# The second layer's mixer of an fp32 block net in a written order, with PSUM tiles and more weights prepared ahead

## Chip, cores, metric

One core of a Trainium2 chip (trn2). The metric is the device time of one execution of the program in microseconds; lower is better.

## What is computed

The input x is 256 tokens by 1024 channels, in fp32. A first block has two layers, each a mixer and an MLP with a residual, and a second block with two kinds of attention follows. The change touches the MLP of the first layer (called MLP 0) and the mixer of the second (called layer 1), so only these are shown:

```python
def rg_lru(x, w_r, b_r, w_i, b_i, lam):
    r = sigmoid(einsum("bshi,hij->bshj", xb, w_r) + b_r)   # 8 heads of 128
    i = sigmoid(einsum("bshi,hij->bshj", xb, w_i) + b_i)
    log_a = -8 * r * softplus(-lam)
    a = exp(log_a)
    bx = sqrt(-expm1(2 * log_a)) * (i * x)
    return scan over tokens of h = a * h_before + bx

def mixer_c(h, w_in, conv_w, conv_b, w_r, b_r, w_i, b_i, lam, w_out):
    gate, xr = split(h @ w_in, 2)
    xr = causal_depthwise_conv(xr, conv_w) + conv_b        # 4 taps
    y = rg_lru(xr, ...) * gelu(gate)
    return y @ w_out

def sq_relu_mlp(h, w_up, w_down):
    return square(relu(h @ w_up)) @ w_down
```

Ahead of a mixer and an MLP stands an RMS norm of x.

## The kernel before

**Products.** Channels lie on partitions, tokens on the free axis. Each fp32 operand is a high half (rounded to the engine's fp32r) and a low half (the rest), and a product is three matmuls of 128x128 by 128x256 (`mm3`): high weight by high input (L360), high weight by low input (L361), low weight by high input (L362).

**Weight units.** The weights are 243 units of 128x1024 (512 KB) in the order in which PE uses them (`weight_plan`, L70). SP issues their transfers into four tiles `raw`, one after the other; a transfer waits until the unit four before has been read for the last time. `ready` (L312) and `prep` (L304) then make the high half (a copy on ACT, L307, or on DVE, L309) and the low half (a subtraction on DVE or POOL, L310). `POLICY` (L44) names the two engines by kind of unit, "a", "v" and "g" for ACT, DVE and POOL: "ag" is the high half on ACT and the low half on POOL. The halves go into a ring of `RING` = 6 buffers `wh` and `wl` and, between layer 0 and the middle of MLP 1, `EXTRA` = 4 more, `wxh` and `wxl`. `unit(name, ahead)` (L341) hands out the next unit and prepares so many beyond it as `ahead` says: 2, and from step 10 of MLP 0 on `FAR` = 6. Each engine executes its own instructions in order; a scheduler places them where the program leaves it free, so that in layer 1 pieces of several products are interleaved on PE.

**MLP 0** has 16 steps: an up product of 256 columns, relu and square, and from the third step on two rows of the down product. Its last rows and its end are `proj_tail` (L818): for each of four column blocks the last 4 rows, the residual x, its high half scaled by the gain (`xsh`, ACT, L841), its low half (`xsl`, DVE, L847) and its square (L855); the squares are added up in `s1` (DVE, L857), and POOL folds the two halves of `s1` (L861).

**Layer 1** (`layer1`, L987) has 26 units of 24 matmuls: 8 `xr`, 2 `ri` (the gates' weights of four heads each), 8 `cg` (the gelu branch), 8 `wo1` (the output, one row of 128 input channels each). `gfirst` (L376) multiplies the first four xr units; between, two columns of matmuls sum `s1` over partitions (L424), and POOL computes the inverse root `rc` (L435) from which PE and ACT spread `R` over the partitions (L442, L448). The two halves of the squares' sum are needed there. The product with R gives xr (DVE, L1034); ACT starts the convolution (L1038), DVE adds three taps (L1042), the last into an SBUF tile `xc`, and each head is split into `xch` (ACT, L399) and `xcl` (DVE, L407) in two buffers. `ri(u)` multiplies them; ACT makes the two gates (L1018, L1019) from a PSUM tile `acc`, and then a second tanh and the decay's exponential (L1022, L1023); DVE squares the decay (L1026). Then come the root (L1057), the gelus (L1050), DVE's scans (L1064), the product with the gelu (L1066) and the split of the result into `xr` (ACT, L399) and `ysl` (DVE, L407), and the output rows. Its first five rows are multiplied row by row, the last three in `proj_tail`. The scheduler is held by one rule only: roots after the last exponential, gelus after the roots (`issue_after`).

Of the kernel before, what the change touches and what calls it, by code (L numbers as in the profile page):

```python
# [17 lines left out]
T = 256  # L18
# [9 lines left out]
EXTRA = 4  # L28
FAR = 6
# [15 lines left out]
POLICY.update(val=("av", "ag", "av", "ag"), gate=("av", "av", "av", "ag"), xr=("av", "ag"), ri=("vg",), cg=("vg",))  # L45
POLICY["wo0"] = ("ag",) * 7 + ("av",)
POLICY["up"] = ("ag",) * 4 + ("av",) * 60
POLICY["wo1"] = ("ag",) * 2 + ("av",) * 6
# [21 lines left out]
def weight_plan(I):  # L70
# [48 lines left out]
    ri(1)  # L119
    for j in range(8):  # L120
        inn("cg", w, j * 128)
# [127 lines left out]
class Kern:  # L249
# [11 lines left out]

    def pool(self, name, space=None):
        return self.tc.tile_pool(name=name, bufs=1) if space is None else \
            self.tc.tile_pool(name=name, bufs=1, space=space)
# [47 lines left out]
    def ready(self):  # L312
# [26 lines left out]
        self.q.append((name, (wh, wl)))  # L339

# [477 lines left out]
    def proj_tail(self, acc, name, ins, gname, g0, xs, R2=None, mp=None, sums=(), after=None):  # L818
# [4 lines left out]
        with self.tc.issue_after(after.ins) if after else nullcontext():  # L823
            ws = [self.unit(name) for _ in ins]
        n = len(ins)
        late = []
        for b in range(4):
# [17 lines left out]
            if xs is not None:  # L845
                for k in ks:
                    V.scalar_tensor_tensor(xs[1][:, k], x[:, k], g[k % 2], xs[0][:, k].bitcast(F32),  # L847
                                           op0=ALU.mult, op1=ALU.subtract)
            for i, (st, scaled) in enumerate(sums):
# [10 lines left out]
        for st, _ in sums:  # L860
            G.tensor_tensor(st[:, 0], st[:, 0], st[:, 1], op=ALU.add)  # L861

    def mod_setup(self, mp):
# [4 lines left out]
        tv = self.t(mp, [128, 2048], "tv")  # L868
# [118 lines left out]
    def layer1(self, lp):  # L987
# [8 lines left out]
        xc = self.t(lp, [128, 8, T], "xc")  # L996
# [4 lines left out]
        parts = [self.s1[:, 0]]  # L1001
        rc = []
        self.ahead = 2
# [3 lines left out]
        def ri(u):  # L1007
            w = self.unit("ri")
            hs = range(4 * u, 4 * u + 4)
            for h in hs:  # L1010
                xch = self.t(lp, [128, T], "xch", F32R, bufs=2)
                xcl = self.t(lp, [128, T], "xcl", F32R, bufs=2)
                self.split(xc[:, h], xch, xcl)
                ps = self.ps("acc")
                for i in range(2):
                    c = slice(((h % 4) * 2 + i) * 128, ((h % 4) * 2 + i + 1) * 128)
                    self.mm3(ps[:, i * T:(i + 1) * T], (w[0][:, c], w[1][:, c]), (xch, xcl), True, True)
                S.activation(r[:, h], ps[:, :T], AF.Tanh, bias=hb[:, h:h + 1], scale=0.5)  # L1018
                S.activation(ig[:, h], ps[:, T:], AF.Tanh, bias=hb[:, 8 + h:9 + h], scale=0.5)  # L1019
                V.scalar_tensor_tensor(ig[:, h], ig[:, h], 1.0, xc[:, h], op0=ALU.add, op1=ALU.mult)  # L1020
            for h in hs:
                S.activation(th[:, h], r[:, h], AF.Tanh, scale=sp[:, h:h + 1], bias=sp[:, h:h + 1])  # L1022
                last = S.activation(r[:, h], r[:, h], AF.Exp, scale=nsp[:, h:h + 1], bias=nsp[:, h:h + 1])  # L1023
                if h % 2:
                    sl = slice(h - 1, h + 1)
                    V.tensor_tensor(xc[:, sl], r[:, sl], r[:, sl], op=ALU.mult)  # L1026
                    V.scalar_tensor_tensor(th[:, sl], xc[:, sl], 1.0, th[:, sl], op0=ALU.add, op1=ALU.mult)
            return last

        for p in range(4):  # L1030
            if 2 * p == RI0:
                ri(0)
            ps = pss[p] if p < 2 else self.gpair(("xr", "xr"), xs)
            V.tensor_tensor(xr[:, 2 * p:2 * p + 2, 3:], self.pair(ps), self.b2(R), op=ALU.mult)  # L1034
            ca = self.pair(self.ps("acc"))
# [3 lines left out]
            for i in range(3):  # L1039
                for h in range(2):  # L1040
                    j = 2 * p + h
                    V.scalar_tensor_tensor(xc[:, j] if i == 2 else ca[:, h], xr[:, j, i:i + T],  # L1042
                                           self.p("ccw", j * 4 + i), ca[:, h], op0=ALU.mult, op1=ALU.add)

        def gate_pair(p):
            ps = self.gpair(("cg", "cg"), xs)
            xg = gl[:, 2 * p:2 * p + 2]
            V.tensor_tensor(xg, self.pair(ps), self.b2(R), op=ALU.mult)
            with self.tc.issue_after(sq.ins):
                S.activation(xg, xg, AF.Gelu_apprx_tanh)  # L1050

        ex = ri(1)
        ys = (self.t(lp, [128, 8, T], "xr", F32R), ysl)
        sls = [slice(4 * b, 4 * b + 4) for b in range(2)]
        for sl in sls:
            with self.tc.issue_after(ex.ins):
                sq = S.activation(th[:, sl], th[:, sl], AF.Sqrt, scale=0.25)  # L1057
        for p in range(4):
            gate_pair(p)
        for b, sl in enumerate(sls):  # L1060
            V.tensor_tensor(ig[:, sl], ig[:, sl], th[:, sl], op=ALU.mult)
            for p in (2 * b, 2 * b + 1):
                for h in (2 * p, 2 * p + 1):
                    V.tensor_tensor_scan(xc[:, h], r[:, h], ig[:, h], 0.0, op0=ALU.mult, op1=ALU.add)  # L1064
                hp = slice(2 * p, 2 * p + 2)
                V.tensor_tensor(xc[:, hp], xc[:, hp], gl[:, hp], op=ALU.mult)  # L1066
                self.split(xc[:, hp], ys[0][:, hp], ys[1][:, hp])
        acc = [self.ps("acc") for _ in range(4)]
        for k in range(5):
            self.krow(acc, self.unit("wo1"), (ys[0][:, k], ys[1][:, k]), k == 0, False)  # L1070
        xs = self.new_h()
# [462 lines left out]
```

## Time and profile before

| what | us |
|---|---|
| median of 3 executions | 831.25 |
| lowest, highest | 829.29, 834.26 |
| the profiled execution | 829.35 |
| its span | 827.5 |

Of the span PE (matmul) was busy 790.3 us, 96%; DVE 71%, ACT 55%, POOL 27%. The mean granted clock of TensorE was 0.987 of full speed. The rows below are of that execution; times count from the start of its span. MLP 0 ends and layer 1 begins on PE at 292 us, and layer 1 ends at 385 us. A row of a table by stretch names the stretch, then for each engine its busy time and the number of its instructions. A row of waits names the engine and line that waits, what it waits for, and how long.

### The profile page before, as it was taken

The numbers are of one execution on the slowest core, as the hardware profiler recorded it, in microseconds if no ns is written. First come the engines' busy times: TensorE is split into PE (matmuls) and PEld (weight loads), VectorE is DVE, ScalarE is ACT, GpSimd is POOL, SyncE is SP. The second block draws the span as 40 slices with busy tenths as digits, with TensorE's granted clock in tenths as the row PEclk, the third lists the DMA queues.
The fourth block names the chain that finished last, engine by engine and source line by source line (L and its number), as shares of the span: only waits on it lengthen the run. The fifth ranks groups of instructions, "written<-read, shape, count | busy, mean of one in ns | idle before, by whom it ended". The sixth has DMA issues, their size and how long they took to land.

```text
span 827.5 us, 16152 instructions
## 1 busy us (share of the span) xinstructions
PE 790.3 (96%) x6476; PEld 757.8 (92%) x6476; DVE 589.2 (71%) x956; ACT 457.4 (55%) x722; POOL 220.6 (27%) x160
## 2 busy tenths in 40 slices
PE   6999899999999978798999999999999999999996
PEld 6997799999999978698999999999989988889996
DVE  6899659999997698898638445557634877566743
ACT  5578546544446625576636444545626587765433
POOL 4886634110111465500441101111000022220001
PEclk9999999999999999799999999999999999999998
DMA  7864357878878744318646566665234532554621
GB/s 237 305 204 128 102 179 240 336 269 301 289 275 280 250 120 136 112 49 303 222 126 202 185 183 201 191 194 177 85 126 142 165 104 101 179 166 166 204 78 51
DMA packets 41259, 152.32 MB, mean 184 GB/s; under 512 B 4576, under 2 KB 5088, under 8 KB 39008
## 3 DMA queue, kind: packets, MB, share of 16 engines
q1 hardware_dynamic: 40752, 149.19, 55.4%
q10 hardware_dynamic: 432, 2.10, 0.6%
q8 instruction: 51, 0.84, 0.4%
q14 instruction: 24, 0.20, 0.1%
HBM read 149.17 MB, written 2.10 MB: 183 GB/s over the span
## 4 chain that ended last, share of the span: by engine, by line
PE 74%; DVE 11%; ACT 5%; DMA 3%; issue 3%; POOL 2%; SPq 0%; POOLq 0%; DVEq 0%; ACTq 0%
PE mm L360 13%; PE mm L361 13%; PE mm L362 12%; PE acc L361 10%; PE acc L360 9%; PE acc L362 9%; DMA raw<-in_wst 3%; PE acc L1320 2%; PE acc L1348 2%; PE mm L1357 2%; DVE wl L310 2%; ACT wh L307 1%; DVE ysl L407 1%; POOL wl L310 1%; PE mm L442 1%
## 5 line engine op out<-in xcount | busy, mean ns | idle before, releaser
L307 ACT ACTIVATE wh<-raw 128x1024 fp32r<-128x1024 f32 (+1 forms) x198 | 207.1, 1049 | 185.6 <-PE mm L361 77.3
L310 DVE TENSOR_TENSOR wl<-raw,wh 128x1024 fp32r<-128x1024 f32 (+1 forms) x167 | 208.8, 1257 | 109.5 <-ACT wh L307 109.4
L361 PE MATMUL mm<-xsl,wh 128*128 128x256 f32 x824 | 229.7, 279 | 1.5 <-DVE xsl L847 1.5
L360 PE MATMUL mm<-xsh,wh 128*128 128x256 f32 x824 | 231.0, 280 | 0.0
L362 PE MATMUL mm<-xsh,wl 128*128 128x256 f32 x824 | 229.6, 279 | 0.0
L360 PEld LDWEIGHTS mm<-xsh,wh 128*128 128x128 f32 x824 | 156.0, 189 | 3.7 <-issue 3.3
L361 PEld LDWEIGHTS mm<-xsl,wh 128*128 128x128 f32 x824 | 156.0, 189 | 2.6 <-DVE xsl L847 2.1
L362 PEld LDWEIGHTS mm<-xsh,wl 128*128 128x128 f32 x824 | 155.6, 189 | 0.0
L957 POOL TENSOR_TENSOR ma<-mr 128x512 f32<-128x512 f32 x32 | 49.7, 1554 | 233.7 <-ACT mr L955 233.7
L361 PE MATMUL acc<-mal,wh 128*128 128x256 f32 x384 | 106.6, 278 | 0.7 <-DVE mal L407 0.7
L360 PE MATMUL acc<-mah,wh 128*128 128x256 f32 x384 | 106.7, 278 | 0.0
L362 PE MATMUL acc<-mah,wl 128*128 128x256 f32 x384 | 106.3, 277 | 0.0
L310 POOL TENSOR_TENSOR wl<-raw,wh 128x1024 fp32r<-128x1024 f32 x36 | 87.9, 2463 | 27.9 <-ACT wh L307 27.2
L361 PEld LDWEIGHTS acc<-mal,wh 128*128 128x128 f32 x384 | 72.4, 188 | 1.3 <-DVE mal L407 1.3
L362 PEld LDWEIGHTS acc<-mah,wl 128*128 128x128 f32 x384 | 72.1, 188 | 0.0
L360 PEld LDWEIGHTS acc<-mah,wh 128*128 128x128 f32 x384 | 72.1, 188 | 0.0
L307 ACT ACTIVATE wxh<-raw 128x1024 fp32r<-128x1024 f32 x35 | 36.6, 1056 | 34.7 <-DMA raw<-in_wst 27.0
L883 DVE CUSTOM_DVE_ANT_0 mdump<-mw,cv 128x1024 f32<-128x1024 f32 x40 | 51.0, 1274 | 3.4 <-DMA mw<-in_modw 3.1
L310 DVE TENSOR_TENSOR wxl<-raw,wxh 128x1024 fp32r<-128x1024 f32 x34 | 43.7, 1305 | 9.4 <-ACT wxh L307 9.4
L361 PE MATMUL mm<-xsl,wxh 128*128 128x256 f32 x168 | 47.5, 283 | 1.9 <-DVE xsl L847 1.9
L360 PE MATMUL mm<-xsh,wxh 128*128 128x256 f32 x168 | 47.6, 284 | 0.2 <-ACT xsh L841 0.2
L362 PE MATMUL mm<-xsh,wxl 128*128 128x256 f32 x168 | 47.2, 281 | 0.0
(374 smaller groups left out, 1765.1 us busy)
## 6 DMA issues: line engine op xcount, KB each, us to landing
raw<-in_wst SPq DMA_DIRECT2D x240, 512.0 KB, 4.1
mw<-in_modw SPq DMA_DIRECT2D x12, 1024.0 KB, 7.5
nb<-in_nab SPq DMA_DIRECT2D x16, 256.0 KB, 3.6
ab<-in_alibi ACTq DMA_DIRECT2D x1, 1536.0 KB, 7.8
x<-in_xT SPq DMA_DIRECT2D x4, 256.0 KB, 5.2
cv<-in_cvec SPq DMA_DIRECT2D x1, 1024.0 KB, 4.7
cx<-in_cT SPq DMA_DIRECT2D x1, 1024.0 KB, 6.5
xd<-x SPq DMA_DIRECT2D x1, 1024.0 KB, 4.4
```

The costliest lines, as they stand in the source:

```text
L307: nc.scalar.activation(wh, r, AF.Copy)
L310: (nc.vector if lo == "v" else nc.gpsimd).tensor_tensor(wl, r, wh.bitcast(F32), op=ALU.subtract)
L360: mm(out, w[0], x[0], start=start, stop=False, skip_group_check=True)
L361: mm(out, w[0], x[1], start=False, stop=False, skip_group_check=True)
L362: return mm(out, w[1], x[0], start=False, stop=stop, skip_group_check=True)
L407: self.nc.vector.tensor_tensor(l, src, h.bitcast(F32), op=ALU.subtract)
L442: self.lasts = self.nc.tensor.matmul(ps[:, j * 128:(j + 1) * 128], rc[:, j:j + 1].to_broadcast([128, 128]), self.ident, start=True, stop=True)
L883: V.tensor_tensor_reduce(d, w, cv[:, s * 1024:(s + 1) * 1024], 0.5, 0.0, op0=ALU.mult, op1=ALU.add, accum_out=self.mod[:, s * 24 + i:s * 2 ...
L957: G.tensor_tensor(a, r, r, op=ALU.mult)
L1320: PE.matmul(sc[i], Q[tag, h][a][:, qs], K[tag, h][b], start=a + b == 0, stop=a == 1)
L1348: PE.transpose(pt[:, i * 128:(i + 1) * 128], P[:, i * 128:(i + 1) * 128], self.ident)
L1357: PE.matmul(o[64 * hh:64 * hh + 64, :T], vt[:, i, h * 64:h * 64 + 64], PTs[tag, h][:, i], start=i == 0, stop=i == 3, skip_group_check=True)
```

## The change

- `EXTRA` goes from 4 to 6 buffers and `FAR` from 6 to 11 units, so that up to eleven units can be ready when MLP 0 ends. In the tail the units are taken with fewer ahead, and `fill(n)`, a new function that prepares until n units are waiting, sets how many are prepared at each place.
- `ri` and every second `cg` and `wo1` change engines: all 26 high halves of layer 1 are ACT's. The second `ri` unit stands behind the first two cg units.
- POOL's fold of `s1` is left out in MLP 0, and the sum over partitions takes both halves (4 matmuls of one column instead of 2).
- `layer1` is written as steps in a fixed order. `inorder` chains each PE and each ACT instruction of layer 1 to the one before it, so the scheduler can't exchange them. The convolved heads stay in the PSUM tiles `acc` (no `xc`), `xch` and `xcl` have four buffers, the gates' products go into `mm` tiles, the decay is squared by ACT into PSUM, root and gelu come in two halves (5 table loads instead of 2).

```diff
-EXTRA = 4
-FAR = 6
+EXTRA = 6
+FAR = 11
...
-POLICY.update(val=("av", "ag", "av", "ag"), gate=("av", "av", "av", "ag"), xr=("av", "ag"), ri=("vg",), cg=("vg",))
+POLICY.update(val=("av", "ag", "av", "ag"), gate=("av", "av", "av", "ag"), xr=("av", "ag"), ri=("ag",), cg=("ag", "av"))
...
-POLICY["wo1"] = ("ag",) * 2 + ("av",) * 6
+POLICY["wo1"] = ("ag", "av")
...
-    ri(1)
     for j in range(8):
+        if j == 2:
+            ri(1)
         inn("cg", w, j * 128)
...
+    @contextmanager
+    def inorder(self, *engines):
+
+        traced = self.nc.cur_bb.bb.instructions
+        old = {id(i) for i in traced}
+        yield
+        last = {}
+        for i in traced:
+            if id(i) not in old and i.engine in engines:
+                if i.engine in last:
+                    self.tc.add_manual_dep(i, last[i.engine].name, mybir.DependencyInfo(
+                        mybir.DependencyClass.NoSync, mybir.DependencyReason.DATA), reason="issue_after")
+                last[i.engine] = i
...
+    def fill(self, n):
+
+        while len(self.q) < n and self.u < N_UNITS:
+            self.ready()
...
-            ws = [self.unit(name) for _ in ins]
+            ws = [self.unit(name, len(ins) - 1 - i) for i in range(len(ins))]
...
+            self.fill(min(1 + b, 3))
...
-        for st, _ in sums:
+        for st, _ in sums if mp and xs is None else ():
...
-        tv = self.t(mp, [128, 2048], "tv")
+        tv = self.t(mp, [128, 2048], "mw", bufs=2)
...
-        xc = self.t(lp, [128, 8, T], "xc")
...
-        parts = [self.s1[:, 0]]
+        parts = [self.s1[:, 0], self.s1[:, 1]]
         rc = []
-        self.ahead = 2
+        self.ahead = 0
+        PIN = (PE.engine, S.engine)
...
-            ca = self.pair(self.ps("acc"))
+            ca = cas[p] = self.pair(self.ps("acc"))
...
-                    V.scalar_tensor_tensor(xc[:, j] if i == 2 else ca[:, h], xr[:, j, i:i + T],
+                    V.scalar_tensor_tensor(ca[:, h], xr[:, j, i:i + T],
...
+        def heads(p):
+            for h in (2 * p, 2 * p + 1):
+                sp3[h] = (self.t(lp, [128, T], "xch", F32R, bufs=4), self.t(lp, [128, T], "xcl", F32R, bufs=4))
+                self.split(cas[p][:, h % 2], *sp3[h])
+
+        def ri(u):
+            w = self.unit("ri")
+            out = []
+            for h in range(4 * u, 4 * u + 4):
+                ps = self.ps()
+                for i in range(2):
+                    c = slice(((h % 4) * 2 + i) * 128, ((h % 4) * 2 + i + 1) * 128)
+                    self.mm3(ps[:, i * T:(i + 1) * T], (w[0][:, c], w[1][:, c]), sp3[h], True, True)
+                out.append(ps)
+            return out
+
+        def gates(u, pr):
+            for h in range(4 * u, 4 * u + 4):
+                ps = pr[h % 4]
+                S.activation(r[:, h], ps[:, :T], AF.Tanh, bias=hb[:, h:h + 1], scale=0.5)
+                S.activation(ig[:, h], ps[:, T:], AF.Tanh, bias=hb[:, 8 + h:9 + h], scale=0.5)
+                V.scalar_tensor_tensor(ig[:, h], ig[:, h], 1.0, cas[h // 2][:, h % 2], op0=ALU.add, op1=ALU.mult)
+
+        def tanhs(u):
+            for h in range(4 * u, 4 * u + 4):
+                S.activation(th[:, h], r[:, h], AF.Tanh, scale=sp[:, h:h + 1], bias=sp[:, h:h + 1])
+
+        def decay(p):
+            for h in (2 * p, 2 * p + 1):
+                S.activation(r[:, h], r[:, h], AF.Exp, scale=nsp[:, h:h + 1], bias=nsp[:, h:h + 1])
+            sl = slice(2 * p, 2 * p + 2)
+            a2 = self.pair(self.ps("acc"))
+            S.activation(a2, r[:, sl], AF.Square)
+            V.scalar_tensor_tensor(th[:, sl], a2, 1.0, th[:, sl], op0=ALU.add, op1=ALU.mult)
+
+        def root(u):
+            sl = slice(4 * u, 4 * u + 4)
+            S.activation(th[:, sl], th[:, sl], AF.Sqrt, scale=0.25)
+            for p in (2 * u, 2 * u + 1):
+                hp = slice(2 * p, 2 * p + 2)
+                V.tensor_tensor(ig[:, hp], ig[:, hp], th[:, hp], op=ALU.mult)
+                for h in (2 * p, 2 * p + 1):
+                    V.tensor_tensor_scan(th[:, h], r[:, h], ig[:, h], 0.0, op0=ALU.mult, op1=ALU.add)
+
...
+
+        def gelu(p):
+            S.activation(gl[:, 2 * p:2 * p + 2], gl[:, 2 * p:2 * p + 2], AF.Gelu_apprx_tanh)
+
+        def done(p):
+            hp = slice(2 * p, 2 * p + 2)
+            V.tensor_tensor(th[:, hp], th[:, hp], gl[:, hp], op=ALU.mult)
+            self.split(th[:, hp], ys[0][:, hp], ys[1][:, hp])
+
+        def wrow(k):
             self.krow(acc, self.unit("wo1"), (ys[0][:, k], ys[1][:, k]), k == 0, False)
+
+        with self.inorder(*PIN):
+            conv(0, pss[0])
+            self.fill(5)
+            conv(1, pss[1])
+            self.fill(6)
+            p2 = self.gpair(("xr", "xr"), xs)
+            heads(0)
+            heads(1)
+            r0 = ri(0)
+            self.fill(5)
+            conv(2, p2)
+            gates(0, r0)
+            self.fill(7)
+            tanhs(0)
+            p3 = self.gpair(("xr", "xr"), xs)
+            self.fill(7)
+            conv(3, p3)
+            decay(0)
+            self.fill(8)
+            decay(1)
+            cg(0)
+            heads(2)
+            heads(3)
+            self.fill(8)
+            gates(1, ri(1))
+            root(0)
+            self.fill(8)
+            cg(1)
+            ys = (self.t(lp, [128, 8, T], "xr", F32R), ysl)
+            gelu(0)
+            gelu(1)
+            done(0)
+            tanhs(1)
+            self.fill(8)
+            cg(2)
+            done(1)
+            decay(2)
+            decay(3)
+            self.fill(8)
+            cg(3)
+            root(1)
+            gelu(2)
+            gelu(3)
+            self.fill(7)
+            acc = [self.ps("acc") for _ in range(4)]
+            for k in range(4):
+                wrow(k)
+                self.fill(7)
+            done(2)
+            done(3)
+            wrow(4)
+        self.ahead = 2
```

Three places show how the instructions move.

POOL, from the end of MLP 0 on. `wxl` and `wl` are low halves of weights, `s` is `s1`, `rc` the inverse root. Before:

```order
L310 TENSOR_TENSOR wxl_3590<-raw_3587,wxh_3589 128x1024
L310 TENSOR_TENSOR wxl_3881<-raw_3878,wxh_3880 128x1024
L995 MEMSET xr_3739 128x8x3
L310 TENSOR_TENSOR wl_3951<-raw_3948,wh_3950 128x1024
L861 TENSOR_TENSOR s_5_76<-s_5_76 128x256
L310 TENSOR_TENSOR wl_4026<-raw_4023,wh_4025 128x1024
L310 TENSOR_TENSOR wl_4056<-raw_4053,wh_4055 128x1024
L435 TENSOR_TENSOR rc_3820<-var_3818,mhalf_85 128x2
L310 TENSOR_TENSOR wl_4096<-raw_4093,wh_4095 128x1024
```

After:

```order
L978 TENSOR_TENSOR ma_3524<-mr_3523 128x512
L325 TENSOR_TENSOR wxl_3568<-raw_3565,wxh_3567 128x1024
L1016 MEMSET xr_3744 128x8x3
L455 TENSOR_TENSOR rc_3826<-var_3824,mhalf_85 128x2
L325 TENSOR_TENSOR wxl_3882<-raw_3879,wxh_3881 128x1024
L325 TENSOR_TENSOR wxl_3898<-raw_3895,wxh_3897 128x1024
```

Ahead of `rc` stood five low halves and the fold, now one low half; those of xr 7 and of the first cg unit come behind it.

PE at the first product of `ri(0)`. `mm` tiles of `xsh`, `xsl` are the xr product, `xch` and `xcl` the convolved heads. Before:

```order
L360 MATMUL mm_618_4022<-xsh_557_3567,wh_604_3950 128x256
L361 MATMUL mm_618_4022<-xsl_558_3568,wh_604_3950 128x256
L362 MATMUL mm_618_4022<-xsh_557_3567,wl_605_3951 128x256
L361 MATMUL acc_608_3958<-xcl_607_3955,wxh_597_3880 128x256
L362 MATMUL acc_608_3958<-xch_606_3954,wxl_598_3881 128x256
L360 MATMUL acc_608_3958<-xch_606_3954,wxh_597_3880 128x256
L361 MATMUL acc_608_3958<-xcl_607_3955,wxh_597_3880 128x256
L362 MATMUL acc_608_3958<-xch_606_3954,wxl_598_3881 128x256
L361 MATMUL acc_611_3972<-xcl_610_3969,wxh_597_3880 128x256
L362 MATMUL acc_611_3972<-xch_609_3968,wxl_598_3881 128x256
```

After:

```order
L380 MATMUL mm_606_3901<-xsh_572_3597,wxh_564_3533 128x256
L381 MATMUL mm_606_3901<-xsl_573_3598,wxh_564_3533 128x256
L382 MATMUL mm_606_3901<-xsh_572_3597,wxl_565_3534 128x256
L380 MATMUL mm_615_3966<-xch_607_3950,wxh_569_3567 128x256
L381 MATMUL mm_615_3966<-xcl_608_3951,wxh_569_3567 128x256
L382 MATMUL mm_615_3966<-xch_607_3950,wxl_570_3568 128x256
```

Before, the first matmul of head 0 went out ahead of others of xr 6, and the rest followed between them; now the heads come in one piece right behind xr 5, and xr 6 and 7 behind all four heads.

ACT at the end of layer 1. `th` and `gl` are the roots and gelus, `xr` from `th` the split of the result, two channel rows of wo1 each. Before:

```order
L1057 ACT_TABLE_LOAD
L1057 ACTIVATE th_3744<-th_3744 128x1024 x2
L1050 ACT_TABLE_LOAD
L1050 ACTIVATE gl_3746<-gl_3746 128x512 x3
L307 ACTIVATE wh_4480<-raw_4478 128x1024
L399 ACTIVATE xr_4167<-xc_3742 128x512
L307 ACTIVATE wh_4510<-raw_4508 128x1024
L399 ACTIVATE xr_4167<-xc_3742 128x512
L307 ACTIVATE wh_4540<-raw_4538 128x1024
L307 ACTIVATE wxh_4570<-raw_4568 128x1024
L399 ACTIVATE xr_4167<-xc_3742 128x512
L1050 ACTIVATE gl_3746<-gl_3746 128x512
L399 ACTIVATE xr_4167<-xc_3742 128x512
```

After:

```order
L322 ACTIVATE wxh_4399<-raw_4397 128x1024
L322 ACTIVATE wh_4405<-raw_4403 128x1024
L1079 ACT_TABLE_LOAD
L1079 ACTIVATE th_3748<-th_3748 128x1024
L1091 ACT_TABLE_LOAD
L1091 ACTIVATE gl_3750<-gl_3750 128x512 x2
L322 ACTIVATE wh_4470<-raw_4468 128x1024
L322 ACTIVATE wh_4504<-raw_4502 128x1024
L322 ACTIVATE wh_4534<-raw_4532 128x1024
L322 ACTIVATE wh_4564<-raw_4562 128x1024
L322 ACTIVATE wh_4594<-raw_4592 128x1024
L419 ACTIVATE xr_4312<-th_3748 128x512 x2
```

Before, one or two high halves stood between two splits; now five stand in one piece between the last gelus and the splits for rows 4 to 7.

## Rows read from the trace of the kernel before

**Rows 1.** Busy time by stretch: layer 1, and its last part without pauses.
```profile
core 0: us, PE busy (x) PEld busy (x) DVE busy (x) ACT busy (x) POOL busy (x), PEclk, DMA share, GB/s
292.00:385.00 93.00, 79.75 (x632) 77.11 (x631) 80.62 (x107) 48.62 (x83) 35.63 (x16) 0.93 0.43 133
349.00:385.00 36.00, 35.97 (x318) 35.77 (x317) 30.42 (x40) 24.86 (x33) 0.00 (x0) 1.00 0.42 138
```

**Rows 2.** Waits of PE, 280 to 385 us: total, times, longest.
```profile
PE acc L361 <- DVE xcl L407: 7.7, 4, 5.1
PE mm L442 <- POOL rc L435: 3.0, 1, 3.0
PE mm L361 <- DVE xsl L847: 1.5, 1, 1.5
PE mm L424 <- POOL s L861: 0.6, 1, 0.6
```

**Rows 3.** Busy time by stretch, columns as in rows 1: behind two pauses.
```profile
310.00:315.00 5.00, 5.00 (x33) 5.00 (x31) 2.26 (x4) 2.58 (x5) 5.00 (x3) 0.66 0.52 165
345.00:350.00 5.00, 5.00 (x33) 5.00 (x33) 2.71 (x5) 4.28 (x10) 0.00 (x0) 0.70 0.13 47
```

**Rows 4.** Timeline of POOL: start, length, operation, [idle before <- releaser].
```profile
302.23 5.61 POOL L310 TENSOR_TENSOR wl<-raw,wh 128x1024 fp32r<-128x1024 f32 x2
307.80 1.68 POOL L435 TENSOR_TENSOR rc<-var,mhalf 128x2 f32<-128x2 f32 x1
317.04 2.40 POOL L310 TENSOR_TENSOR wxl<-raw,wxh 128x1024 fp32r<-128x1024 f32 x1 [0.68 <-issue]
```

**Rows 5.** Timeline of DVE, columns as in rows 4.
```profile
292.73 4.64 DVE L847 SCALAR_TENSOR_TENSOR xsl<-x,par,xsh 128x256 fp32r<-128x256 f32 x2
320.36 0.68 DVE L1034 TENSOR_TENSOR xr<-mm,R 128x512 f32<-128x512 f32 x1
338.12 0.48 DVE L1042 SCALAR_TENSOR_TENSOR acc<-xr,par,acc 128x256 f32<-128x256 f32 x1
338.51 2.17 DVE L407 TENSOR_TENSOR xcl<-xc,xch 128x256 fp32r<-128x256 f32 x1
358.61 1.85 DVE L1064 TENSOR_TENSOR_SCAN xc<-r,ig 128x256 f32<-128x256 f32 x3
372.08 1.23 DVE L310 TENSOR_TENSOR wxl<-raw,wxh 128x1024 fp32r<-128x1024 f32 x1
```

**Rows 6.** Timeline of ACT, columns as in rows 4.
```profile
310.36 0.39 ACT L448 ACTIVATE R<-mm 128x256 f32<-128x256 f32 x1 [10.97 <-PE mm L442]
321.07 1.17 ACT L1038 ACTIVATE acc<-xr,par 128x256 f32<-128x256 f32 x2 [0.58 <-DVE xr L1034]
330.01 0.47 ACT L1018 ACTIVATE r<-acc,hb 128x256 f32<-128x256 f32 x1
330.36 0.48 ACT L1019 ACTIVATE ig<-acc,hb 128x256 f32<-128x256 f32 x1
333.80 2.00 ACT L307 ACTIVATE wh<-raw 128x1024 fp32r<-128x1024 f32 x2
352.23 1.09 ACT L1023 ACTIVATE r<-r,sm 128x256 f32<-128x256 f32 x2
353.34 1.28 ACT L1057 ACT_TABLE_LOAD   x1
354.63 2.01 ACT L1057 ACTIVATE th<-th 128x1024 f32<-128x1024 f32 x2
357.96 1.68 ACT L1050 ACTIVATE gl<-gl 128x512 f32<-128x512 f32 x3
```

**Rows 7.** DMA issues: times, KB each, median us to landing.
```profile
raw<-in_wst SPq DMA_DIRECT2D x240, 512.0 KB, 4.1
```

**Rows 8.** Busy time by stretch, columns as in rows 1: the end of MLP 0.
```profile
250.00:280.00 30.00, 30.00 (x267) 30.00 (x266) 20.03 (x18) 20.95 (x24) 9.51 (x5) 1.00 0.84 272
```

**Rows 9.** Waits of PE, 385 to 400 us, columns as in rows 2.
```profile
PE mm L361 <- DVE xsl L847: 1.9, 3, 0.9
```

## What the change will do to the time, and why

> **What bounds the kernel now.** The page's first part comes first; by it PE is the engine that is busy nearly all the time, so time can only be won where PE pauses or runs at the lower clock. The table of busy time by stretch then shows where: in layer 1, from 292 to 385 us, PE issued 632 matmuls, was busy 79.75 of 93.00 us, and the granted clock was 0.93; in the stretch 349 to 385 it issued 318 in 36 us without a pause, 0.113 us each [rows 1]. Layer 1 has 26 weight units of 24 matmuls, 624, which is 70.6 us at that pace; the few small ones of the norm take another 0.9. So 93.0 - 71.5 = 21.5 us are lost there. PE's waits name 12.8 of them: 7.7 for the low half of the convolved heads (`xcl`), 3.0 for `rc`, 1.5 for the low half of the residual (`xsl`) and 0.6 for the fold `s` [rows 2]. After the 3.0 us wait the clock was 0.66 for five microseconds, 33 matmuls where 44 would fit; after the 5.1 us wait the same is seen again in 345 to 350 [rows 3]. That is the clock's lower level (1.2 instead of 2.4 GHz) after a pause. It cost 11 x 0.113 = 1.3 us the first time and about twice that the second, 4 in all. The rest, 4.7 us, is short gaps.
>
> What is late in these waits? POOL's rows: two low halves queued (5.61 us) ahead of `rc` [rows 4]. DVE's rows: two `xsl` of 128x256 took 4.64 us while POOL ran low halves, and one `xcl` 2.17 us, where an operation with its operand in PSUM, the convolution's tap, took 0.48 beside POOL [rows 5]. So layer 1 waits for DVE and POOL hindering each other, and for POOL's order.
>
> **What the change takes away.** At the start of layer 1 POOL has no low half and no fold of the square sums left, only the memset and `rc`. The waits for `xsl` (1.5), for the fold (0.6) and for `rc` (3.0) go, and with the last the 1.3 at the lower clock: 6.4 us. The convolved heads now stay in PSUM and most low halves are done elsewhere: the `xcl` waits (7.7) and the 2.7 at the lower clock go: 10.4 us. The short gaps sat between interleaved pieces that no longer exist; I count their 4.7 as gone. Together 21.5 us.
>
> **What it costs: new waits, because PE and ACT are pinned.** ACT now makes all high halves, the squares, and five table loads instead of two, in a written order, and PE cannot pull other work forward. I walk ACT and DVE through that order with the durations of [rows 5, 6]: gate tanhs start 0.36 apart, second tanhs and exponentials 0.5 (1.09 for two), conv starts 1.17 a pair, high halves 1.0, gelus 0.56 and the splits of the same tile 0.6, square roots 1.0, loads 1.28.
> (a) `ri(0)` stands right behind xr 4 and 5. From R to the first `xcl`: R 0.4, product 0.68, conv starts 1.17, high half 1.0, low half 1.23, six taps 2.4, `xch` 0.4, then two taps, a product and `xcl` 1.8: 9.1 us with the hand-overs; PE has 48 matmuls, 5.4. Wait 3.7, and 1.1 more for the other heads: 4.8.
> (b) xr 6 and 7 need a PSUM tile that `ri(0)` holds until its first gates; ACT has two high halves, two conv starts and two gates ahead, 4.0, PE 1.2: 2.7.
> (c) `ri(1)` needs `xch` of head 4, behind 7 gates 2.5, five high halves 5.0, 4 tanhs 2.0, conv starts 1.17, exponentials 2.0, squares 1.2, split 0.4: 14.3, against 96 matmuls, 10.9. With `xcl` and the next heads 4.6.
> (d) cg 2 waits like (b): 2.8 against 1.1, 1.7.
> (e) wo1's first row needs a tile that DVE frees after the second decay, 2.3.
> (f) wo1's row 4 needs `done(2)`'s split. ACT from the gate of head 4: 7 gates 2.5, five loads 6.4, square roots 2.0, gelus 2.2, tanhs and exponentials 4.0, squares 1.1, five high halves 5.0, two splits 1.2: 24.4; in it a wait of 2.9 for DVE's four scans (0.62 each), products and a low half. Behind the last gelu stand five more high halves. The fifth can't start before the raw tile of the first is free: high half 1.0, low half on POOL 2.4 [rows 4], transfer 4.1 [rows 7], high half 1.0, low half on DVE 1.2, `ysl` 0.7: 10.4. Together 37.7 us; PE has 240 matmuls, 27.1, and (e): 29.4. Wait 8.3.
> Sum 24.4 us. At the lower clock I add 2.0: after 3.0 us of pause 1.3 was lost, after 5.1 us 2.7 [rows 3]; what follows (a) is swallowed by (b), what follows (f) isn't. So layer 1 loses 26.4 instead of 21.5: +4.9.
>
> **Beside it.** At MLP 1's start PE now waits 1.9 for `xsl` [rows 9], because the first up units arrive there late; after the change seven lie ready, and I take 1.9 and a small gap of 0.2 as gone (other end: they stay, nothing won). The five more units prepared in MLP 0 need 2.6 MB over the 65 us from 215 to 280, 40 GB/s beside 272 at a DMA share of 0.84 [rows 8], and 3 DVE low halves; SP issues their transfers in the one queue of the weights, each when the raw tile four units back is free. At that pace a full share would be 272 / 0.84 = 324, so 52 are free for the 40. PE waits for nothing there, so I cost them at nothing. If that cover fails, the cost is rival 4 below. Two more matmuls of one column in the norm: under 0.3 us.
>
> **The sum**: 829.35 (the profiled execution; 1.9 under the median of 831.25) + 4.9 - 2.1 = 832.1. The forecast is 832.0, no change that can be told (0.5% is 4.2 us). Its own range is 828.5 to 835.5.
>
> A page of the Trainium skill speaks against this change: ScalarE: Activation LUTs, section What ACT_TABLE_LOAD costs, gives about 1.28 us for a load and 1.38 for a drain at every switch. The row has 1.28 for the load, and the square root begins at 354.63, 0.01 after the load's end [rows 6], so the trace shows no drain; by the page the five loads would cost 6.9 more, and the sum would be 839.0.
>
> **The rivals.**
> 1. ACT arrives early, **faster**. If ACT reaches its last gelu 8 us sooner than my chain says, (f) and the lower clock behind it vanish: 832.1 - 8.3 - 2.0 = 821.8. For it: ACT was busy only 48.6 of 93 us [rows 1]; 12 more high halves, 3 loads and 4 squares make it 67, so it has room, and my chains let every link start as late as possible. Against it: the chain of (f) is bound by one raw tile, a POOL low half and a transfer, each measured. Each microsecond that ACT gains is one for the kernel, down to that value.
> 2. The lower clock, **slower**. If the pause before `ri(0)` acts like the one of 5.1 us, PE runs xr 6 and 7 at half pace: 48 x 0.113 = 5.4 us later for conv 3, which stands in ACT's pinned chain with about one microsecond to spare. Then everything up to (f) shifts by 4.4, and the sum is 836.5. [...] For it: three pauses of over 3 us follow one another; against it: (b) covers half of the first.
> 3. Each table load stops ACT for as long again as the load itself: five times 1.28 = 6.4 in chain (f), 838.5. Against it are the 0.01 us between load and square root. The page named above has this rule.
> 4. MLP 0 can't prepare eleven units, because the transfers are near what they do: then layer 1 starts with few, POOL and DVE meet again in the transition, and the 6.4 come back: 838.5. Against it are the 52 GB/s free.
>
> **How the numbers follow.** Forecast 0.38, rival 1 0.30, rival 2 0.23, rival 3 0.04, rival 4 0.05. Faster is rival 1, 0.30; slower are the last three and the upper edge of the forecast, 0.34; 0.36 remains for no change. The range goes from 820 (rival 1 less a little) to 839 (rivals 3 and 4); it leaves out the tails of the two large cases, two in ten.
>
> **What would show it.** Right: no PE wait for `rc` or `xsl` in the transition, `R` made at about 304 us instead of 310.4 [rows 6]; pauses of 3 to 5 us at the first matmul with `xch` and `xcl`; the largest pause, 6 to 9 us, on the split of wo1's rows 4 and 5 with ACT's fifth high half waiting for a transfer; MLP 1 starting at 387 to 391. Wrong: a pause on POOL in the transition (rival 4), a gap behind each table load (rival 3), clock under 0.7 between 310 and 335 (rival 2), or no pause at wo1's row 4 (rival 1).

## Result and profile after

| | before | after |
|---|---|---|
| median, us | 831.03 (20 executions) | 836.95 (20 executions) |
| lowest, highest | 826.25, 834.74 | 831.30, 842.31 |
| the profiled execution, its span | 829.35, 827.5 | 838.86, 837.1 |

The change makes the kernel slower: 5.9 us, a ratio of 1.007 with an interval of 1.0052 to 1.0089. The first part of the page of the kernel after:

```profile
span 837.1 us, 16157 instructions
PE 793.6 (95%) x6480; PEld 761.5 (91%) x6480; DVE 576.5 (69%) x946; ACT 473.9 (57%) x739; POOL 213.9 (26%) x157
```

The two profiled executions are 9.6 us of span apart, the medians 5.9, since one profile lies 1.9 above its median and the other 1.7 below. Where the 9.6 arise is read from the starts of the same matmuls in both traces. 1.9 are there before the order differs anywhere, so they are chance. MLP 0 adds 6.4 between its second and its last down row. From that last row to the first down row of MLP 1 it is 113.44 us against 113.27: **layer 1 and the start of MLP 1 together add only 0.2**. Behind it come another 1.2, and then nothing more. So the loss lies in a stage that I had priced at nothing, and the rewritten layer breaks even.

The waits of PE from 236 to 397 us after the change (engine, line, what it waits for: total, times, longest), which answer to [rows 2]:

```profile
PE acc L380 <- ACT xr L419: 5.5, 1, 5.5
PE mm L380 <- ACT xch L419: 4.6, 2, 2.4
PE acc L381 <- DVE mal L427: 3.1, 2, 2.7
PE mm L381 <- DVE xcl L427: 2.4, 2, 1.5
PE mm L380 <- ACT ig L1062: 2.4, 1, 2.4
PE acc L380 <- DVE th L1075: 2.2, 2, 1.6
PE acc L381 <- DVE ysl L427: 0.8, 1, 0.8
```

`rc`, `s` and `xsl` have gone, as was foretold, also at the start of MLP 1 [rows 9]. In their place stand waits for the pinned chains, 17.9 us without `mal`. `mal`, the low half of MLP 0's squared relu, is new at this size. In the same view of before it has this row:

```profile
PE acc L361 <- DVE mal L407: 0.2, 1, 0.2
```

Busy time by stretch after the change, columns as in [rows 1]; the first answers to [rows 8], and the last two to [rows 3]:

```profile
250.00:280.00 30.00, 30.00 (x257) 30.00 (x256) 21.48 (x24) 19.62 (x22) 9.67 (x6) 1.00 0.78 263
289.00:293.00 4.00, 3.94 (x20) 3.94 (x21) 1.30 (x3) 0.00 (x0) 0.00 (x0) 0.57 0.46 135
320.00:325.00 5.00, 3.66 (x21) 2.89 (x22) 3.66 (x9) 2.30 (x5) 1.94 (x1) 1.00 0.65 218
345.00:350.00 5.00, 5.00 (x36) 5.00 (x35) 3.11 (x6) 4.98 (x11) 2.50 (x1) 0.77 0.35 108
385.00:390.00 5.00, 5.00 (x32) 5.00 (x32) 3.46 (x4) 2.87 (x3) 0.00 (x0) 0.68 0.96 318
```

The granted clock is the mean of a stretch. It falls to its lower level (1.2 GHz) for a part of the stretches behind the `mal` wait (289), behind the second pause of the heads (345) and behind the one of row 4 (385), but not behind `ri(0)`'s pauses (320 to 325, 1.00).

**The wait at the end of MLP 0.** The timeline of POOL after the change, there and late in layer 1 (start, length, operation, [idle before <- releaser]):

```profile
282.18 2.98 POOL L325 TENSOR_TENSOR wxl<-raw,wxh 128x1024 fp32r<-128x1024 f32 x1 [0.37 <-ACT wxh L322]
285.12 1.04 POOL L978 TENSOR_TENSOR ma<-mr 128x512 f32<-128x512 f32 x1
286.12 2.34 POOL L325 TENSOR_TENSOR wxl<-raw,wxh 128x1024 fp32r<-128x1024 f32 x1
...
375.73 2.49 POOL L325 TENSOR_TENSOR wl<-raw,wh 128x1024 fp32r<-128x1024 f32 x1 [4.34 <-ACT wh L322]
```

The timeline of ACT, the same columns, at that place, at R and ahead of row 4:

```profile
282.01 0.58 ACT L976 ACTIVATE mr<-mm 128x512 f32<-128x512 f32 x1
...
312.83 0.39 ACT L468 ACTIVATE R<-mm 128x256 f32<-128x256 f32 x1 [9.11 <-PE mm L462]
...
372.25 1.28 ACT L1091 ACT_TABLE_LOAD   x1
373.54 1.16 ACT L1091 ACTIVATE gl<-gl 128x512 f32<-128x512 f32 x2
374.61 3.89 ACT L322 ACTIVATE wh<-raw 128x1024 fp32r<-128x1024 f32 x4
381.67 1.06 ACT L322 ACTIVATE wh<-raw 128x1024 fp32r<-128x1024 f32 x1 [3.18 <-DMA raw<-in_wst]
382.63 1.14 ACT L419 ACTIVATE xr<-th 128x512 fp32r<-128x512 f32 x2
```

The timeline of DVE, the same columns, in the middle of MLP 0 and at its end:

```profile
242.08 1.22 DVE L904 CUSTOM_DVE_ANT_0 mdump<-mw,cv 128x1024 f32<-128x1024 f32 x1 [4.38 <-DMA mw<-in_modw]
...
286.20 2.81 DVE L427 TENSOR_TENSOR mal<-ma,mah 128x512 fp32r<-128x512 f32 x1 [3.30 <-POOL ma L978]
```

The last of these rows, as it was at the same place before:

```profile
281.65 0.69 DVE L407 TENSOR_TENSOR mal<-ma,mah 128x512 fp32r<-128x512 f32 x1 [3.30 <-POOL ma L957]
```

The last relu `mr` is ready at 282.59. POOL could square it then, but a low half (`wxl`, of a unit prepared for layer 1) stands in front and holds POOL until 285.16: 2.6 us. The square's low half `mal` is DVE's and starts at 286.20, while POOL has begun the next low half, and takes 2.81 instead of the 0.69 before. PE's timeline shows the outcome, and the pauses of layer 1 with it:

```profile
289.06 0.45 PE L381 MATMUL acc<-mal,wxh 128*128 128x256 f32 x1 [2.70 <-DVE mal L427]
...
320.36 0.38 PE L380 MATMUL mm<-xch,wxh 128*128 128x256 f32 x1 [2.19 <-ACT xch L419]
321.65 0.38 PE L381 MATMUL mm<-xcl,wxh 128*128 128x256 f32 x1 [0.91 <-DVE xcl L427]
321.87 0.29 PE L382 MATMUL mm<-xch,wxl 128*128 128x256 f32 x1
321.99 0.28 PE L380 MATMUL mm<-xch,wxh 128*128 128x256 f32 x1
...
383.30 0.58 PE L380 MATMUL acc<-xr,wxh 128*128 128x256 f32 x1 [5.48 <-ACT xr L419]
```

Against before, by the starts of the same matmuls, that is 2.5 us of gap and 1.6 behind it at the lower clock. The rest of the 6.4 in MLP 0 is not of the same certainty: DVE waited 4.38 us for the modulation's data, with `mal` behind it in the queue, PE paused 0.4 at 245 and lost 0.7 there in all, and from there to 286 its matmuls came 0.118 us apart instead of 0.1135 (257 in 30 us instead of 267), 1.5 us.

A page of the Trainium skill bears on `mal`: GPSIMD Engine Reference, section 1. Specifications, says that POOL shares its SBUF interfaces with VectorE, with contention for DVE instructions that have two SBUF inputs. The trace agrees: 2.81 us against 0.69, and `mal` has two.

### The profile page after: what moved, and what is told of

The parts are those of the page before. It is cut to its first block, busy times and chain, and to the rows that moved or that the text cites. A ratio compares the mean times of both kernels' runs of the same rounds, so it can differ in the third digit from the quotient of the medians.

```text
span 837.1 us, 16157 instructions
## 1 busy us (share of the span) xinstructions
PE 793.6 (95%) x6480; PEld 761.5 (91%) x6480; DVE 576.5 (69%) x946; ACT 473.9 (57%) x739; POOL 213.9 (26%) x157
## 4 chain that ended last, share of the span: by engine, by line
PE 52%; ACT 5%; DVE 5%; issue 2%; POOL 1%; DMA 0%; POOLq 0%; DVEq 0%; ACTq 0%
PE mm L380 9%; PE mm L381 9%; PE mm L382 9%; PE acc L381 6%; PE acc L382 6%; PE acc L380 6%; PE acc L1402 2%; PE acc L1430 2%; PE mm L1439 2%; ACT wh L322 1%; DVE wl L325 1%; ACT wxh L322 1%; DVE acc L1039 1%; PE mm L462 1%; ACT th L1067 0%
## 5 line engine op out<-in xcount | busy, mean ns | idle before, releaser
L380 PE MATMUL mm<-xsh,wh 128*128 128x256 f32 x808 | 225.9, 280 | 0.0
L381 PE MATMUL mm<-xsl,wh 128*128 128x256 f32 x808 | 224.4, 278 | 0.0
L382 PE MATMUL mm<-xsh,wl 128*128 128x256 f32 x808 | 224.3, 278 | 0.0
L381 PE MATMUL acc<-mal,wh 128*128 128x256 f32 x360 | 100.2, 278 | 1.0 <-DVE mal L427 1.0
L380 PE MATMUL acc<-mah,wh 128*128 128x256 f32 x360 | 100.4, 279 | 0.0
L382 PE MATMUL acc<-mah,wl 128*128 128x256 f32 x360 | 100.0, 278 | 0.0
L325 POOL TENSOR_TENSOR wl<-raw,wh 128x1024 fp32r<-128x1024 f32 x33 | 79.7, 2433 | 46.0 <-ACT wh L322 40.8
L322 ACT ACTIVATE wxh<-raw 128x1024 fp32r<-128x1024 f32 x48 | 50.4, 1058 | 40.8 <-DMA raw<-in_wst 36.3
L381 PEld LDWEIGHTS acc<-mal,wh 128*128 128x128 f32 x360 | 68.0, 189 | 1.2 <-DVE mal L427 1.2
L325 DVE TENSOR_TENSOR wxl<-raw,wxh 128x1024 fp32r<-128x1024 f32 x41 | 53.5, 1313 | 7.1 <-ACT wxh L322 6.7
```

The lines of the kernel that those rows point to most:

```text
L322: nc.scalar.activation(wh, r, AF.Copy)
L325: (nc.vector if lo == "v" else nc.gpsimd).tensor_tensor(wl, r, wh.bitcast(F32), op=ALU.subtract)
L380: mm(out, w[0], x[0], start=start, stop=False, skip_group_check=True)
L381: mm(out, w[0], x[1], start=False, stop=False, skip_group_check=True)
L382: return mm(out, w[1], x[0], start=False, stop=stop, skip_group_check=True)
```

## Experiments

The theory behind the first runs (A, where an expectation uses letters): the loss is made in MLP 0, by low halves that the longer preparation puts on POOL ahead of the last squares, and layer 1 only exchanges waits. Its rival: layer 1's written order makes the loss, by ACT's chain.

**1. The last low halves of MLP 0 on DVE** (after, with two units' engines changed):

```diff
-xr=("av", "ag"), ri=("ag",),
+xr=("av", "ag", "av", "ag", "av", "av", "av", "ag"), ri=("av", "ag"),
```

> The low halves of xr 5 and of the first ri unit, the last two that MLP 0 prepares, go from POOL to DVE; nothing else changes. Theory A (POOL's low halves stand ahead of the last `ma` of MLP 0, and PE waits 2.7 us for it and then runs at the lower clock): the wait for `mal` at the end of MLP 0 falls from 2.7 to under 0.5 us, the stretch at half clock behind it (1.3 us) is gone, the time falls by about 4 us, to 833. Theory B (the loss lies in layer 1's pinned order, the wait in MLP 0 was one of the profiled execution): no change, 837. Theory C (the added units' transfers come late, whoever makes the low half): the wait for `mal` stays at 1.5 us or more, now behind DVE's low halves, 836.

Measured: 832.63, ratio 1.002 [0.9999, 1.0040]. POOL's rows at the same place:

```profile
278.37 2.41 POOL L325 TENSOR_TENSOR wl<-raw,wh 128x1024 fp32r<-128x1024 f32 x1 [0.57 <-ACT wh L322]
282.17 1.72 POOL L978 TENSOR_TENSOR ma<-mr 128x512 f32<-128x512 f32 x1 [1.40 <-ACT mr L976]
```

POOL is idle when the last relu comes, and the wait at 286 is gone. In ratio the loss falls from 0.7% to 0.2%: two entries of a table undo 4 to 5 of the 5.9 us. One wait for `mal` is left in PE's waits from 236 to 397 us:

```profile
PE acc L381 <- DVE mal L427: 1.2, 1, 1.2
```

It is the pause at 245, longer here than in after, with the pace of 0.118 us behind it, and MLP 0 is still 3.2 us longer than before's in this profile. POOL's low halves at the end of MLP 0 don't make that pause. Run 2, which differs from after in layer 1 alone, doesn't have it in its profile, nor does run 6; there MLP 0 is 6.2 and 6.3 us longer by the wait at its end and the lower clock behind it. What makes the pause at 245 was not tried.

**2. The last two results finished before the output rows** (after):

```diff
             acc = [self.ps("acc") for _ in range(4)]
+            done(2)
+            done(3)
             for k in range(4):
                 wrow(k)
                 self.fill(7)
-            done(2)
-            done(3)
```

> The two splits for wo1's rows 4 to 7 are written ahead of the four preparations that stand between rows 0 to 3; nothing else changes. If the wait at row 4 is the chain of the prediction's term (f) (high half, low half on POOL, transfer, high half, split), the waits of 5.5 and 0.8 us at row 4 fall to under 2 in all and the 1.5 us at the lower clock behind them go: 6 less in layer 1. Part comes back at MLP 1's start, whose first units are then prepared later: net 3 to 6 less, 831 to 834. Rival: all of it comes back there, because the units' transfers are the limit: 836 to 837.

Measured: 834.23, ratio 1.0037 [1.0013, 1.0060], just above the 831 to 834 expected. The wait at row 4 fell from 5.5 to 1.6 us, MLP 0 still had its `mal` wait (3.6).

**3. Both** (edits 1 and 2).

> Both edits of the two runs before. If they are independent the gains add up: 8 us less, 829, about 2 us below the kernel before. If only theory B holds, as the second run alone; if only A, as the first.

Measured: 830.59, ratio 0.9983 [0.9963, 1.0003]. The two gains add, within the intervals. With these two places mended, what is left is neither faster nor slower than before.

**4. The preparation undone in after.**

```diff
-FAR = 11
+FAR = 6
```

> FAR back from 11 to 6, the rest as in the changed kernel. Theory A: MLP 0's end is as in the kernel before (no wait for `mal` over 0.5 us, no half clock: 5 to 6 us less there), but four or five units more are prepared by ACT in the transition, ahead of the convolved heads: the waits at the first ri unit and at xr 6 grow by 2 to 5 us; in all 833 to 837. Theory B: MLP 0 gives nothing, layer 1 gets longer: 839 to 842.

Measured: 838.98, ratio 1.0093 [1.0057, 1.0129], worse than after. MLP 0 was clean, with no `mal` wait, as the theory says, but layer 1 took 5.8 us longer than before's, more than expected. PE's waits from 236 to 397 us have a new row:

```profile
PE mm L380 <- ACT wh L322: 3.5, 1, 3.5
```

This high half of xr 4 or 5 stands in ACT's written order behind R and the first conv starts, at 306.27; PE could not pull other work ahead. The eleven units are not an extra of the change: the written order needs them.

**5. The preparation alone, in before.**

```diff
-EXTRA = 4
-FAR = 6
+EXTRA = 6
+FAR = 11
...
-        tv = self.t(mp, [128, 2048], "tv")
+        tv = self.t(mp, [128, 2048], "mw", bufs=2)
```

> The kernel before with FAR 11 and EXTRA 6 alone (and the one tile that shares a buffer for it); layer 1 is the old one. POOL then makes the low half of xr 5 ahead of the last `ma` of MLP 0, as in the changed kernel. Theory A: PE waits 2 to 4 us for `mal` at the end of MLP 0 and runs some 3 us at half clock behind it, although nothing of the new layer 1 is there; `rc` still waits behind low halves on POOL. Time 834 to 837. Rival (the wait comes from the new tail with its `fill`): no wait for `mal` over 0.5 us, 829 to 831.

Measured: 831.43, ratio 0.9989 [0.9956, 1.0021]. Two of PE's waits from 236 to 397 us:

```profile
PE mm L361 <- DVE xsl L847: 4.6, 2, 4.3
...
PE acc L361 <- DVE mal L407: 1.8, 1, 1.8
```

The `mal` wait is there without the new layer 1 (MLP 0 is 4.8 us longer), a little under what was expected. But the old layer 1 gained 3.0 from the units ready, so the time did not rise clear of the noise: I had expected 834 to 837. The `xsl` wait stayed, which speaks against my assumption that it goes with the units ready alone.

**6. The order left to the scheduler** (after).

```diff
-        PIN = (PE.engine, S.engine)
+        PIN = ()
```

> The changed kernel with the pins taken out (no engine is held to the written order in layer 1). The scheduler then puts the splits for row 4 ahead of the fifth high half and 8 table loads instead of 5. If the pinned order is what costs layer 1 its waits: the wait at row 4 goes from 6.3 to under 3 us, the heads' waits shrink, 831 to 834. Rival (the same chains of work are behind the waits in any order): 836 or more, with three loads of 1.28 us added.

Measured: 832.87, ratio 1.0016 [0.9984, 1.0047]. With 8 table loads instead of 5, layer 1 is still 4.6 us shorter than after's in the profiles; the `mal` wait (3.7) stands. The pins cost about 4 us.

**7. Another written order** (on 3): `ri(0)` behind all xr units, `ri(1)` before cg 4, the products apart from the conv starts; the core of the edit:

```diff
-            conv(0, pss[0])
+            prod(0, pss[0])
+            prod(1, pss[1])
+            conv(0)
+            conv(1)
...
+            prod(2, self.gpair(("xr", "xr"), xs))
+            prod(3, self.gpair(("xr", "xr"), xs))
             heads(0)
             heads(1)
             r0 = ri(0)
```

> On top of the second of the two edits combined before: the first ri unit moves behind all xr units and the second behind cg 3, with the steps of ACT in that order. PE then has 96 matmuls (10.9 us) instead of 48 over the 9.1 us to the first `xcl`. If term (a) of the prediction is a chain of that length, the waits at the first `xch` and `xcl` (2.2 and 1.2 us) fall to under 1, and the one at xr 6 turns into one at cg 0 of 1 to 3; the second ri unit waits less than 3. Layer 1 is 3 to 6 us shorter than in the combined kernel: 825 to 828. Rival: ACT's chain to row 4 sets the end, the waits only move to row 4: 830.

Measured: 833.43, ratio 1.0016 [0.9988, 1.0044]: a miss. The heads' waits went, and these rows of PE's waits came:

```profile
PE mm L379 <- ACT ig L1063: 9.2, 2, 7.8
PE acc L379 <- DVE th L1076: 4.0, 1, 4.0
```

The wait moved to the product that needs the gates' PSUM tile, since the gates of the second ri unit stand in ACT's order behind two decays and three high halves, the last of which waited 1.28 us for its transfer (340.76 in ACT's timeline; the gates start at 341.73, the product at 342.60).

**8. Where did the old layer 1 lose its 21.5?** Only the engines of two kinds of unit, in before:

```diff
-ri=("vg",), cg=("vg",))
+ri=("av",), cg=("av",))
```

> The kernel before, but the units ri and cg take the high half from ACT and the low half from DVE, so that POOL makes no low half in most of layer 1. If the waits for `xcl` (7.7 us) come from POOL and DVE hindering each other, they fall to under 3 and the clock stays up in 340 to 348; layer 1 gets 5 to 9 us shorter, 822 to 827. Rival: DVE's ten low halves more (1.2 each) are as late as the hindered operations were, and the time stays at 829 to 833.

Measured: 818.06, ratio **0.9834 [0.9778, 0.9889]**, far more than expected: layer 1 is 13.8 us shorter. PE's waits from 280 to 385 us:

```profile
PE acc L361 <- DVE xcl L407: 2.0, 2, 1.8
...
PE mm L424 <- POOL s L861: 1.2, 1, 1.2
```

`rc` has gone and `xcl` fell from 7.7 [rows 2]. The two have different reasons. `rc` is a matter of POOL's queue: the two low halves ahead of it [rows 4] are no longer there, and it starts when its own input is ready, as POOL's timeline shows:

```profile
302.92 1.64 POOL L435 TENSOR_TENSOR rc<-var,mhalf 128x2 f32<-128x2 f32 x1 [0.94 <-DVE var L430]
```

`xcl` is a matter of DVE, whose groups in layer 1 (busy, mean ns | idle before) show why. Before:

```profile
L407 DVE TENSOR_TENSOR xcl<-xc,xch 128x256 fp32r<-128x256 f32 x8 | 6.7, 857 | 0.4 <-ACT xch L399 0.4
L847 DVE SCALAR_TENSOR_TENSOR xsl<-x,par,xsh 128x256 fp32r<-128x256 f32 x4 | 5.5, 1415 | 0.0
L1026 DVE TENSOR_TENSOR xc<-r 128x512 f32<-128x512 f32 x4 | 4.7, 1169 | 0.2 <-ACT r L1023 0.2
```

The same view of this run:

```profile
L407 DVE TENSOR_TENSOR xcl<-xc,xch 128x256 fp32r<-128x256 f32 x8 | 5.4, 679 | 0.0
...
L847 DVE SCALAR_TENSOR_TENSOR xsl<-x,par,xsh 128x256 fp32r<-128x256 f32 x8 | 3.5, 477 | 0.1
...
L1026 DVE TENSOR_TENSOR xc<-r 128x512 f32<-128x512 f32 x4 | 2.7, 685 | 0.1
```

The same operations take on the mean 0.48 instead of 1.4 us and 0.69 instead of 1.17 once POOL leaves them alone. Where POOL has a low half left (330.39, 2.37 us), the `xcl` beside it took 2.54 in this run too, where the one ahead of it took 0.41. DVE's timeline:

```profile
330.50 2.54 DVE L407 TENSOR_TENSOR xcl<-xc,xch 128x256 fp32r<-128x256 f32 x1
```

From 292 to 385 the clock stayed at 1.00, as the row of the busy time by stretch shows (MLP 1 begins at 372 in it):

```profile
292.00:385.00 93.00, 86.71 (x725) 84.30 (x724) 83.12 (x123) 67.44 (x109) 13.61 (x8) 1.00 0.53 175
```

PE issued 725 matmuls there instead of 632 [rows 1], and POOL was busy 13.6 us instead of 35.6; ACT took on the high halves, 67.4 instead of 48.6. That DVE lost ten high halves is no rival: it got ten low halves for them and was busy 83.1 us in the stretch instead of 80.6.

**9. The fold of the squares left out as well** (8, and the sum over partitions takes both halves):

```diff
-        for st, _ in sums:
+        for st, _ in sums if mp and xs is None else ():
...
-        parts = [self.s1[:, 0]]
+        parts = [self.s1[:, 0], self.s1[:, 1]]
```

> On top of the run in which ri and cg leave POOL: POOL's fold of s1 is left out in MLP 0 and the sum over partitions takes both halves, as in the change. The wait for the fold (1.2 us there) goes and `rc` comes about 1 us earlier: 816 to 818. Rival: nothing, because `xsl` of the last block ends at the same time: 818.

Measured: 816.25, ratio **0.9806 [0.9759, 0.9853]**, the lowest median of all, 1.9% under before and well under after; the wait for `s` is gone. That it gains on run 8 is not shown: the intervals overlap, and layer 1 takes 99.7 us in its profile and 99.5 in that of run 8.

**10. POOL out of the new layer 1** (after).

```diff
-xr=("av", "ag"), ri=("ag",), cg=("ag", "av"))
+xr=("av", "ag", "av", "ag", "av", "av", "av", "av"), ri=("av",), cg=("av",))
...
-POLICY["wo1"] = ("ag", "av")
+POLICY["wo1"] = ("av",)
```

> The changed kernel with the low halves of ri, cg, wo1 and of the last two xr units on DVE, so that POOL makes none behind MLP 0's end; order and pins as in the change. If what was left of the loss was still POOL against DVE, the time falls as far as the old order did with the same edit, to 818 to 821. If it is ACT's pinned chain, only MLP 0's 4 us and the 1 to 3 us of the POOL low half in term (f) go: 829 to 832, with the waits at the heads and at xr 6 as before.

Measured: 834.05, ratio 1.0034 [1.0002, 1.0066], above both ranges expected. MLP 0 was clean (+0.6) and layer 1 was not faster (+2.3): ACT's chain is the bound there, not DVE beside POOL.

**11. That with edit 2.**

> The same with the splits for rows 4 to 7 ahead of the preparations between rows 0 and 3. If ACT's chain is the bound: 3 us less than the run before, 826 to 829, and still over the old order with POOL out (818). If POOL was: no difference to the run before.

Measured: 830.40, ratio 0.9984 [0.9956, 1.0012], the same as 3, a little above what was expected.

**12. That (10) with the order left to the scheduler,** as in 6.

> The changed kernel with POOL out of layer 1 and with the pins taken out, so that the scheduler orders PE and ACT. If the pins are what holds the new layer 1 above the old one, the waits at the heads, at xr 6 and at row 4 shrink and the time comes near the old order with the same engines (816 to 820). If the new steps themselves are (all splits from PSUM, ri in one piece behind 48 matmuls, more table loads), it falls by no more than the 4 us that the pins cost with POOL in: 828 to 832.

Measured: 823.09, ratio 0.9901 [0.9871, 0.9932], 11 us under run 10 with nothing but the pins gone. PE's waits are left at the heads alone:

```profile
PE mm L380 <- ACT xch L419: 8.7, 3, 4.3
PE mm L381 <- DVE xcl L427: 0.9, 1, 0.9
```

So the pins cost 11 us once POOL is out, and the other parts of the change (runs 12 and 9 both lack the pins and nearly all of POOL's low halves in layer 1) are still some 7 us behind the old ones, 5.6 of them in layer 1 by the two profiles.

## Why the prediction came out as it did

The time, 836.95, lies in the range, but beyond the forecast's own 828.5 to 835.5, and the case that I held likeliest, no change, did not come. That it lies in the range is luck: the range reaches up to 839 for rivals 3 and 4, and 836.5 is what rival 2 gives, but none of their mechanisms is what happened in the kernel after. By terms:

- **What goes, 21.5.** Right in its large parts: no wait for `rc`, `s` or `xsl`, and R comes 12.7 us behind MLP 0's last row (300.09) instead of 18.6 (291.81): 5.8 earlier, where I had 6.4. The short gaps, 4.7, did not all go. Layer 1 alone still loses about 23.7 (21.5 + 0.2 + some 2 won at MLP 1's start); 17.9 of waits and 3.0 at the lower clock leave 2.8.
- **The new waits, 24.4.** Over-priced, at the places named: (a) 3.1 for 4.8, (b) 2.4 for 2.7, (c) 3.9 for 4.6, (d) none for 1.7, (e) 2.2 for 2.3, (f) 6.2 for 8.3; 17.9 in all. Chains that let every link start late give the upper end. That (f) is bound by a raw tile is seen in ACT's rows above: four high halves, then 3.18 us for a transfer, then the split, behind POOL's low half at 375.73.
- **The lower clock, 2.0.** In layer 1 it came twice, behind (c) and (f), some 15 matmuls each at 0.2125 instead of 0.1135 us: 1.5 each, 3.0.
- **MLP 1's start, 2.1 won.** PE's last wait is the one at 384.64, and none follows until 414, so the 1.9 are won.
- **"PE waits for nothing there, so I cost them at nothing": this step failed.** I weighed the five units in MLP 0 against the transfers and counted three low halves on DVE, but did not walk the others through POOL's queue, where the squares of MLP 0 stand and which [rows 8] show busy for only 9.5 of 30 us. What counts is not that share but what stands ahead of one instruction whose result PE needs at once. Run 1 shows that it is this: move those low halves, and 4 to 5 us return. Layer 1 and MLP 1's start together, +2.8 in the sum (4.9 - 2.1), came out at +0.2; without the cost in MLP 0 the sum, 832.1, would have been too high by the over-priced waits. The miss of one term hid that of the other.
- **The rivals.** 1 (ACT early) did not come; its twelve more high halves are ten by the two `POLICY` lines (2 ri, 8 cg), which changes nothing here; run 2 reaches part of its gain by moving the splits. 2 (the clock behind `ri(0)`) did not come in after, but did in run 3, below; of its three pauses of over 3 us the second, (b), had 2.7 in the sum and came out at 2.4. 3 has no support: the gelus start 0.01 us after the load's end (372.25 + 1.28, 373.54). The Trainium skill (ScalarE: Activation LUTs, What ACT_TABLE_LOAD costs) gives a drain of 1.38 us per switch; here as before none is seen. 4 had the right sign, about the right price and nearly the place, but not the mechanism: the transfers kept up (a DMA share of 0.78, units ready at the transition) and POOL's order did the harm.

What the runs settle beyond the prediction: the old layer 1 lost most of its time to POOL's low halves, by `rc` behind them in POOL's queue and by DVE's operations beside them. That run 8 wins by both is shown; how much belongs to each was not tried apart. It needed a line, not a rewrite. The rewrite removed the same loss and bought ACT waits for it. How much of the 7 us between runs 12 and 9 belongs to the PSUM tiles, the split roots, the place of the units or the longer preparation was not tried apart either.

## What to carry to other kernels

When work is moved into a stage with no waits, walk it through the queue of every engine it touches, and look for the one short instruction on which the bound engine depends; a low busy share of that queue says nothing. Before an order is written by hand, try which engine does what: a reassignment of one line gave 1.7% where the written order lost 0.7%, and the scheduler with its freedom did better than the pins by 4 to 11 us. A written order turns every late unit into a stop of the whole chain, so it has to be paid for with more prepared ahead, and that with buffers and queues elsewhere.

## What was not expected of the hardware

**The same pause, with and without a lower clock.** In run 3 the pauses at `ri(0)` are those of after to 0.01 us (2.18 and 0.91 against 2.19 and 0.91 above), and yet PE then ran at half pace for some 15 matmuls, and again from 320.5 on. PE's timeline in run 3:

```profile
312.23 0.38 PE L380 MATMUL mm<-xch,wxh 128*128 128x256 f32 x1 [2.18 <-ACT xch L419]
...
313.52 0.46 PE L381 MATMUL mm<-xcl,wxh 128*128 128x256 f32 x1 [0.91 <-DVE xcl L427]
313.78 0.42 PE L382 MATMUL mm<-xch,wxl 128*128 128x256 f32 x1
314.00 0.41 PE L380 MATMUL mm<-xch,wxh 128*128 128x256 f32 x1
```

Matmuls are 0.22 us apart there against 0.12 in after (321.87, 321.99), and the mean granted clock from 313 to 318 is 0.66, where after has 1.00 behind its pauses. The length of a pause alone doesn't decide; what else does is open. Rival 2 has its place in this.

**Two paces at the full clock.** With a granted clock of 1.00, 30 us held 267 or 268 matmuls in before and in eleven of the runs, and 257 in after and run 1, the two in which PE had paused for `mal` at about 245. So a step is 0.1135 or 0.118 us, and it kept its pace until the next pause: 4%, as much as a wait of 1.2 us in every 30. Why was not tried.
